# First mixer's values computed ahead of its queries and keys, memory statistics moved forward, and twelve weight chunks in products of 512 columns

## The chip, the cores and the metric

One core of a Trainium2 chip runs the whole program. The metric is device microseconds of one launch: the median of 3 runs was 429.3 us before the change (428.47 to 429.76).

## What is computed

One decoder layer on x, 256 tokens by 1024 channels, all in float32, with a memory of 256 tokens:

```
h = rms_norm(x, g_mix);  proj = h @ w_in                  # qa ka va qb kb vb, 512 columns each
oa = rms_norm(moba_attention(qa, ka, va))                 # 8 heads of 64, causal, T5 bias
ob = rms_norm(softmax(q1 k1) - lam * softmax(q2 k2)) @ v  # 4 differential heads
x += concat(oa, ob) @ w_out
m = rms_norm(mem, g_mem)
x += cross_attention(rms_norm(x), m; w_cq, w_ck, w_cv) @ w_co     # 4 heads of 256
x += (silu(rms_norm(x) @ w_gate) * (rms_norm(x) @ w_up)) @ w_down # inner width 2816
out = rms_norm(x, g_final)
```

## The kernel before

**Split products.** Every large product works on float32 data that is split into two parts of the type fp32r: a high part and the rest. A weight chunk is 1 MB. SP loads it into `wr`; ScalarE (ACT) copies it to `wh`, the high part (L124); VectorE (DVE) subtracts to get `wl`, the rest (L109). That is done in four parts of 512 columns per chunk, called parts below, by `wpart` and `wflush`. Three buffers of each kind exist. The activations have a high and a low tile in the same way. TensorE (PE) then forms high by high, high by low and low by high.

**Two shapes of product.** `ws` (L312) keeps a weight block stationary and streams 256 tokens: six products of 256 columns per k-step, eight k-steps per chunk. `ws2` (L321) has the high and low activations side by side and streams both in one product of 512 columns, and the low weight in one of 256: four products per k-step, the sum of the two halves being taken at evacuation. `as_` (L333) keeps activations stationary and streams 512 weight columns; it makes the values (token-major).

**Stages.** In order: start (load x, transpose it, first chunk); the rest of w_in, as qa ka qa ka, values, qb kb qb kb, values; memory keys (w_ck) and half its values; w_out; w_cq; the other memory values; w_co; gate and up (22 chunks); down (11 chunks). The attention of the first two mixers is spread through the w_in chunks.

**The order of work.** The program is one instruction list per engine, executed in that order. `run` emits the k-steps of a chunk; after each step `tick` advances a counter, the slot, emits the work that the table (`at`, `later`) holds for that slot, and by a credit some parts of later weight chunks. So slot 31 is a place in the lists of all engines, and an instruction that waits holds up whatever stands behind it on its engine. One k-step is one slot. Slot 9 comes after the first step of the second chunk. The GpSimd engine (POOL) builds the bias strip with 32 copies (L234), stores it in DRAM, and issues the transfers of the bias (L256), the gains `gvB`, the lambda vectors `lp`, and the memory (L596); these small steps are also in the table.

**Memory.** `mem_load` fetches it on POOL's queue, `mem_stats` (ACT) squares and sums, `mem_scale` (DVE) multiplies in place, `mem_t` (PE) transposes and splits. They stand in slots 32, 52 to 54, 58 to 59 and 61 to 70.

**Start.** The first chunk (qa) is multiplied unsplit in float32 (`wf`, L377) as its pieces arrive, from `hF`, the gained and transposed x; the split tiles `hH`, `hL` are made from `hF` beside it. Before that six products on a zero tile run (`NWARM`, L197).

The slot mechanism in the code:

```
def tick():
    state["slot"] += 1
    for fn, args in todo.pop(state["slot"], ()):
        fn(*args)
...
at(32, mem_load)
...
for t in range(2):
    at(52 + 2 * t, mem_stats, t)
...
at((61, 64, 67, 70)[j], mem_t, j)
```

Of the kernel before, what the change touches and what calls it, by code (L numbers as in the profile page):

```python
# [24 lines left out]
NWARM = 6  # L25
# [12 lines left out]
def layer(ctx: ExitStack, tc: tile.TileContext, x, mem, mix_norm_g, w_in, moba_out_g, diff_lambda,  # L38
# [14 lines left out]

    def acc(name="acc"):
        return ps.tile([P, 2, 256], FT, name=name, tag="acc", bufs=3)
# [17 lines left out]
    for base in (0, 6):  # L73
        qk = [cols(w_in, base + i) for i in range(4)]
        chunks += [qk[0], qk[2], qk[1], qk[3]]
        v0 = 2 if base == 0 else 5
        chunks += [rows(w_in, 0, v0, 4, 512), rows(w_in, 4, v0, 4, 512)]
# [100 lines left out]
    src, (wa_, wb_) = chunks[0]  # L178
    w0 = wpool.tile([P, wa_, wb_], FT, name="wr", tag="wr")
    for xlo, xn_, k, nk in ((0, 256, 0, 2), (256, 256, 2, 2), (512, 512, 4, 2), (0, 0, 6, 2)):  # L180
        if xn_:
            nc.sync.dma_start(xv[:, :, xlo:xlo + xn_], xsrc[:, :, xlo:xlo + xn_])
        nc.sync.dma_start(w0[:, k:k + nk], src[:, k:k + nk])
    raws[0] = w0
    state["dma"] = 1
    wdma(2)
# [145 lines left out]

    def as_(o, a, ka, ts, w, kw, cs, start, stop):  # L333
# [11 lines left out]
    hH, hL = slot(1), slot(2)  # L345
    h = (hH, hL)
    hF = slot(4, FT)
# [10 lines left out]
    def x_gain(k):  # L358

        b = xb[k // 4 * 2 + k % 2][:, k % 4 // 2, :]  # L360
        if k % 2:
            nc.vector.tensor_scalar(hF[:, k, :], b, g(G_MIX + k), None, op0=OP.mult)
        else:
            nc.scalar.activation(hF[:, k, :], b, AF.Copy, scale=g(G_MIX + k))

    def x_split(j):
        ks = slice(2 * j, 2 * j + 2)
        split(hH[:, ks, :], hL[:, ks, :], hF[:, ks, :])
# [5 lines left out]
    def wf(o, w, k):  # L374

        for c in range(2):
            nc.tensor.matmul(o[:, c, :], w[:, k, c * P:(c + 1) * P], hF[:, k, :], start=k == 0 and c == 0,  # L377
                             stop=k == KT - 1, skip_group_check=True)

    RX = {}  # L380

    def x_stats():
        ss = const.tile([P, 2], FT, name="ssx")
        for t in range(2):
            nc.scalar.activation(sq, xv[:, t, :], AF.Square, accum_out=ss[:, t:t + 1])
        RX[1] = rstd(ss, 2, D, "rx")
# [72 lines left out]
    def v_chunk(m):  # L459
        os_ = as_chunks(h)  # L460
# [110 lines left out]
    def mix_t(e2):  # L571

        if "mix" not in M:
            M["mix"] = (slot(1), slot(2))
        mixH, mixL = M["mix"]
# [53 lines left out]
    for t in range(2):  # L629
        at(52 + 2 * t, mem_stats, t)  # L630
    at(56, mem_rstd)
    for t in range(2):
        at(58 + t, mem_scale, t)
# [4 lines left out]
    at(50, heads, "a")  # L638
# [4 lines left out]
    for j in range(4):  # L643
        at((61, 64, 67, 70)[j], mem_t, j)
# [16 lines left out]
    load_g(gvA, 0, 8)  # L661
    o = acc()
    w0 = raws[0]
    state["part"], state["use"], state["done"], state["slot"] = NP, 1, 1, 8

# [3 lines left out]


    busy(1)
    for k in (0, 1):
        x_t(k)
        x_gain(k)
    busy(1)
    wf(o, w0, 0)
    strips()
    x_split(0)
    for k in (2, 3):
        x_t(k)  # L680
        x_gain(k)
    wf(o, w0, 1)
    x_split(1)
    for k in (4, 5):
        x_t(k)
        x_gain(k)
    for k in (2, 3):
        wf(o, w0, k)
    for k in (6, 7):
        x_t(k)  # L690
        x_gain(k)
    x_split(2)
    x_split(3)
    for k in range(4, KT):
        wf(o, w0, k)
    raws.pop(0)
    wdma()
    wpart()
    wflush()
    x_stats()  # L700
    for q in range(NP - 1):
        wpart()
        wflush()
    state["credit"] = -1.0
    for j in range(4):
        at(9 + j, x_keep, j)
    later(6, qk_evac, o, "qa0", True)
# [3 lines left out]
    v_chunk(0)  # L711
# [4 lines left out]
    v_chunk(1)  # L716
# [13 lines left out]
    def cross_ops():  # L730
        return tuple(cx.tile([P, KT, S], FR, name="c" + n, tag="c" + n) for n in "HL")
# [15 lines left out]
    def pair(a, evac, by_k=False, late_kts=(6, 7)):  # L747

        w0, w1 = wuse(), wuse()
        o = [acc(), acc()]  # L750
        early = [k for k in range(KT) if k not in late_kts]
        if by_k:
            run([st for k in early for i, w in enumerate((w0, w1)) for st in ws_steps(o[i], w, a, [k])],
                done=False)
        else:
            for i, w in enumerate((w0, w1)):
                run(ws_steps(o[i], w, a, early), done=False)
        for i, w in enumerate((w0, w1)):
            run(ws_steps(o[i], w, a, late_kts))
            evac(i, o[i])  # L760

    def single(a, evac, i):
        w = wuse()
        o = acc()
        run(ws_steps(o, w, a))
# [26 lines left out]
    h2 = cross_ops()  # L792
# [248 lines left out]
```

## Time and profile before

| what | value |
|---|---|
| median of 3 runs | 429.3 us |
| the profiled execution, its own time | 429.33 us |
| span of its instructions | 427.6 us |
| PE busy | 416.8 us, 97% |
| PE weight loads busy | 382.8 us, 90% |
| DVE busy | 286.4 us, 67% |
| ACT busy | 251.9 us, 59% |
| POOL busy | 27.8 us, 7% |
| mean granted TensorE clock | 0.999 |

The profiled execution took 1.7 us more than its span, and is as good as equal to the median. Busy time counts each instruction from its start to its end; PE's products overlap, so the distance from one start to the next tells more of their rate than their length. Rows name the line, the engine, the operation, the tile written and the tiles read, then shapes and a count; `b` is any of the large activation buffers, the memory's among them.

### The profile page before, as it was taken

The numbers are of one execution on the slowest core, as the hardware profiler recorded it, in microseconds if no ns is written. First come the engines' busy times: TensorE is split into PE (matmuls) and PEld (weight loads), VectorE is DVE, ScalarE is ACT, GpSimd is POOL, SyncE is SP. The second block draws the span as 40 slices with busy tenths as digits, with TensorE's granted clock in tenths as the row PEclk, the third lists the DMA queues.
The fourth block names the chain that finished last, engine by engine and source line by source line (L and its number), as shares of the span: only waits on it lengthen the run. The fifth ranks groups of instructions, "written<-read, shape, count | busy, mean of one in ns | idle before, by whom it ended". The sixth has DMA issues, their size and how long they took to land.

```text
span 427.6 us, 7261 instructions
## 1 busy us (share of the span) xinstructions
PE 416.8 (97%) x2827; PEld 382.8 (90%) x2827; DVE 286.4 (67%) x575; ACT 251.9 (59%) x542; POOL 27.8 (7%) x75
## 2 busy tenths in 40 slices
PE   7989999999999999999999999999999999999994
PEld 4888899989998999998999999999888888888883
DVE  2687848899487667486649678888776766544423
ACT  3677888789565654465546465555656665433312
POOL 4750200000010000000000100000000000000001
PEclk9999999999999999999999999999999999999999
DMA  7987682335538525334633745546863675555002
GB/s 240 325 248 246 176 247 80 135 110 193 192 102 296 193 100 185 112 109 161 193 131 104 254 153 186 187 154 213 279 196 109 193 290 198 198 196 189 9 0 98
DMA packets 58258, 74.61 MB, mean 174 GB/s; under 512 B 1708, under 2 KB 50128, under 8 KB 58224
## 3 DMA queue, kind: packets, MB, share of 16 engines
q1 hardware_dynamic: 56528, 69.87, 50.0%
q0 software_dynamic: 1344, 3.88, 3.1%
q8 instruction: 22, 0.36, 0.3%
q10 hardware_dynamic: 352, 0.40, 0.3%
q14 instruction: 12, 0.10, 0.1%
HBM read 72.50 MB, written 1.64 MB: 173 GB/s over the span
## 4 chain that ended last, share of the span: by engine, by line
PE 81%; DVE 8%; ACT 5%; issue 3%; DMA 2%; POOL 1%; SPq 0%; POOLq 0%; DVEq 0%; ACTq 0%
PE acc L318 30%; PE y L337 13%; PE acc L337 9%; PE att L318 5%; PE acc L326 5%; PE att L326 5%; PE att L327 3%; PE acc L327 3%; DVE wl L109 2%; DMA b<-in_x_dram 2%; PE oc L863 1%; PE att L819 1%; ACT qs L422 1%; PE att L497 1%; DVE b L439 1%
## 5 line engine op out<-in xcount | busy, mean ns | idle before, releaser
L109 DVE TENSOR_TENSOR wl<-wr,wh 128x512 fp32r<-128x512 f32 x256 | 163.5, 685 | 34.6 <-ACT wh L124 34.2
L124 ACT ACTIVATE wh<-wr 128x512 fp32r<-128x512 f32 x256 | 144.9, 621 | 55.1 <-issue 23.8
L318 PE MATMUL acc<-b,wh 128*128 128x256 f32 x672 | 125.0, 286 | 0.0
L318 PEld LDWEIGHTS acc<-b,wh 128*128 128x128 f32 x672 | 104.5, 191 | 0.3
L318 PE MATMUL acc<-b,wl 128*128 128x256 f32 x336 | 95.3, 284 | 1.3 <-DVE wl L109 1.3
L318 PEld LDWEIGHTS acc<-b,wl 128*128 128x128 f32 x336 | 64.2, 191 | 1.9 <-DVE wl L109 1.9
L337 PE MATMUL y<-wh,b 128*128 128x512 f32 x152 | 49.0, 391 | 0.0
L337 PE MATMUL acc<-wh,b 128*128 128x512 f32 x128 | 40.6, 398 | 0.3 <-ACT wh L124 0.3
L326 PE MATMUL acc<-hs,wh 128*128 128x512 f32 x96 | 37.8, 393 | 0.0
L326 PE MATMUL att<-hs,wh 128*128 128x512 f32 x96 | 37.8, 393 | 0.0
L318 PE MATMUL acc<-cH,wh 128*128 128x256 f32 x128 | 36.4, 284 | 0.0
L318 PE MATMUL acc<-cH,wl 128*128 128x256 f32 x128 | 36.2, 283 | 0.0
L318 PE MATMUL acc<-cL,wh 128*128 128x256 f32 x128 | 36.2, 283 | 0.0
L337 PE MATMUL y<-wl,b 128*128 128x512 f32 x88 | 34.2, 389 | 0.0
L337 PEld LDWEIGHTS y<-wh,b 128*128 128x128 f32 x152 | 28.5, 188 | 5.9
L327 PE MATMUL att<-hs,wl 128*128 128x256 f32 x96 | 27.1, 283 | 0.0
L327 PE MATMUL acc<-hs,wl 128*128 128x256 f32 x96 | 27.1, 283 | 0.0
L337 PEld LDWEIGHTS acc<-wh,b 128*128 128x128 f32 x128 | 22.5, 189 | 4.0 <-ACT wh L124 0.5
L337 PE MATMUL acc<-wl,b 128*128 128x512 f32 x64 | 25.2, 394 | 0.0
L318 PEld LDWEIGHTS acc<-cH,wh 128*128 128x128 f32 x128 | 24.2, 189 | 0.3 <-DVE b L310 0.2
L318 PEld LDWEIGHTS acc<-cL,wh 128*128 128x128 f32 x128 | 24.1, 188 | 0.0
L318 PEld LDWEIGHTS acc<-cH,wl 128*128 128x128 f32 x128 | 24.1, 189 | 0.0
(210 smaller groups left out, 626.0 us busy)
## 6 DMA issues: line engine op xcount, KB each, us to landing
wr<-in_w_gate_dram SPq DMA_DIRECT2D x11, 1024.0 KB, 5.1
wr<-in_w_up_dram SPq DMA_DIRECT2D x11, 1024.0 KB, 5.1
wr<-in_w_down_dram SPq DMA_DIRECT2D x11, 1024.0 KB, 4.9
wr<-in_w_in_dram SPq DMA_DIRECT2D x9, 1024.0 KB, 6.4
wr<-in_w_ck_dram SPq DMA_DIRECT2D x4, 1024.0 KB, 4.7
wr<-in_w_cv_dram SPq DMA_DIRECT2D x4, 1024.0 KB, 5.0
wr<-in_w_out_dram SPq DMA_DIRECT2D x4, 1024.0 KB, 4.9
wr<-in_w_cq_dram SPq DMA_DIRECT2D x4, 1024.0 KB, 4.7
```

What stands on the lines that cost most here:

```text
L109: eng.tensor_tensor(l, t, h, op=OP.subtract)
L124: nc.scalar.activation(h, t, AF.Copy)
L318: nc.tensor.matmul(o[:, c, :], m[:, k, cs], b[:, k, :], start=first and c == 0 and q == 0, stop=last and q == 2, skip_group_check=True)
L326: nc.tensor.matmul(o[c], h[:, k, cs], flat(a[:, k]), start=first, stop=last, skip_group_check=True)
L327: nc.tensor.matmul(o[c][:, 0:256], l[:, k, cs], a[:, k, 0, :], start=False, stop=last, skip_group_check=True)
L337: nc.tensor.matmul(o, m[:, ka, ts], b[:, kw, cs], start=start and q == 0, stop=stop and q == 2, skip_group_check=True)
L422: nc.scalar.activation(qs[to, :, r, :], d[half(r)], AF.Copy)
L439: nc.vector.tensor_tensor(ks[half(1 - r), :, r, :], d[half(r)], ks[half(r), :, r, :], op=OP.subtract)
L497: nc.tensor.transpose(b[:, q * P:(q + 1) * P], e[:, q * P:(q + 1) * P], ident)
L819: nc.tensor.matmul(b[:, t, :], a[:, kt, t * P:(t + 1) * P], k[:, kt, :], start=n == 0, stop=n == 5)
L863: nc.tensor.matmul(o[:, dv, :], v[:, mt, cs], p_[:, mt, :], start=n == 0, stop=n == 5)
```

## The change

Five things change together.

1. The order of the w_in chunks becomes values of the first mixer (two chunks), qa ka qa ka, qb kb qb kb, values of the second mixer. The first chunk is now split like the others, part by part between the pieces of x; there is no unsplit product any more. The order of the loads follows: x's second half now comes behind the whole first chunk.
2. `hH`, `hL` and the other activation pairs that `ws2` reads lie side by side in one tile (`both`).
3. The table: the statistics of x at slots 10 and 11, the gains and lambda ahead of the bias loads on POOL, all eight first bias loads by slot 14, the memory load at slot 16, its statistics at 24 to 26, scaling at 29 and 30, transposes at 31 to 36; the first mixer's logits from slot 37, each head's product with the values nine slots later.
4. w_out and w_co (four chunks each) use `ws2`; the residual is added in four DVE operations of 256 columns instead of one of 512.
5. Gate and up chunks use `ws2` from j = 3 on instead of j = 5 (four chunks more), with the scaled activations `scale_h` prepared sooner.

```
-NWARM = 6
+NWARM = 7
...
+    def both(i, dt=FR):
+        return slots.tile([P, KT, 2, S], dt, name=f"b{i}", tag=f"b{i}")
...
+    chunks += v_rows(2) + qk(0) + qk(6) + v_rows(5)
...
+    xdma(0, 256)
+    wkdma(0, 0)
+    xdma(256, 256)
+    for k in range(1, 4):
+        wkdma(0, k)
+    xdma(512, 512)
+    wkdma(1, 0, 2)
+    wkdma(1, 2, 2)
+    state["dma"] = 2
...
+    def x_split(k):
...
+        nc.scalar.activation(hH[:, k, :], b, AF.Copy, scale=g(G_MIX + k))
+        nc.vector.scalar_tensor_tensor(hL[:, k, :], b, g(G_MIX + k), hH[:, k, :], op0=OP.mult, op1=OP.subtract)
...
-    at(13, x_row)
-    at(24, load_g_rest)
-    at(25, load_lambda)
-    at(9, bias_load, 0, 4)
-    at(10, small_loads)
-    at(20, bias_load, 4, 4)
-    at(32, mem_load)
+    for t in range(2):
+        at(10 + t, x_stats, t)
+    at(18, x_row)
+    at(9, small_loads)
+    at(15, load_g_rest)
+    at(20, load_lambda)
+    at(12, bias_load, 0, 4)
+    at(14, bias_load, 4, 4)
+    at(16, mem_load)
     at(45, bias_load, 8, 4)
+    for t in range(2):
+        at(24 + t, mem_stats, t)
+    at(26, mem_rstd)
+    for t in range(2):
+        at(29 + t, mem_scale, t)
+    for j in range(4):
+        at((31, 33, 35, 36)[j], mem_t, j)
     for i in range(8):
-        at(28 + 4 * i, logits, i, i, f"qa{i // 4}", f"ka{i // 4}", i // 2 % 2, i % 2)
-        at(34 + 4 * i, p_t, i)
-        at((51, 52, 53, 54, 56, 59, 63, 67)[i], pv, i, 0, "a", 64)
...
+        n = 4 * i + (37 if i < 4 else 38)
+        at(n, logits, i, i, f"qa{i // 4}", f"ka{i // 4}", i // 2 % 2, i % 2)
+        at(n + 6, p_t, i)
+        at(n + 9, pv, i, 0, "a", 64)
...
     for k in (0, 1):
         x_t(k)
...
     x_split(0)
+    w_split()
+    x_split(1)
+    busy(2)
+    v_now(0)
     for k in (2, 3):
         x_t(k)
...
+    strips()
+    w_split()
+    v_now(1)
+    w_split()
     x_split(2)
     x_split(3)
+    v_now(2)
     for k in range(4, KT):
...
+        x_t(k)
+    w_split()
+    v_now(3)
+    for k in range(4, KT):
+        x_split(k)
...
+    run(v_steps(wuse(), 1, range(4)))
+    later(1, v_evac, 0, os_)
+    qk_chunk("qa0", True)
...
-            nc.vector.tensor_tensor(xs, o, xs, op=OP.add)
+            for c in range(2):
+                for cs in (slice(0, 256), slice(256, 512)):
+                    nc.vector.tensor_tensor(xs[:, c, :], o[c][:, cs], xs[:, c, :], op=OP.add)
...
-        single(M["mix"], ev, i)
...
+        single(M["mix"], ev, i, ws2_steps, two)
...
-    for j in range(5, NFF // 2):
+    for j in range(3, NFF // 2):
```

`v_now(k)` emits the six products of the values with the k-th piece of the first chunk, `w_split` one part of a weight split, `two` one bank of each of the two accumulator groups.

Three places in the instruction lists are spoken of below. The first is POOL's list from the zero fill of the low-query tile (`b_123`, now `b_124`) to the memory load (`b_93`); first the kernel before:

```order
L239 MEMSET b_123 64x2x256 x4
L281 TENSOR_TENSOR rx<-rxv,mhalf 128x2
L256 DMA bias<-strip_d 32x4x256 x4
L245 DMA gvB<-in_cross_norm_g_dram 8x128
L245 DMA gvB<-in_mem_norm_g_dram 8x128
L245 DMA gvB<-in_ffn_norm_g_dram 8x128
L245 DMA gvB<-in_moba_out_g_dram 4x128
L245 DMA gvB<-in_diff_subln_g_dram 1x16x8
L247 DMA lp<-in_diff_lambda_dram 128x256
L256 DMA bias<-strip_d 32x4x256 x4
L596 DMA b_93<-in_mem_dram 128x2x1024
```

The same stretch of POOL's list with the change:

```order
L259 MEMSET b_124 64x2x256 x4
L265 DMA gvB<-in_cross_norm_g_dram 8x128
L265 DMA gvB<-in_mem_norm_g_dram 8x128
L265 DMA gvB<-in_ffn_norm_g_dram 8x128
L265 DMA gvB<-in_moba_out_g_dram 4x128
L265 DMA gvB<-in_diff_subln_g_dram 1x16x8
L267 DMA lp<-in_diff_lambda_dram 128x256
L301 TENSOR_TENSOR rx<-rxv,mhalf 128x2
L276 DMA bias<-strip_d 32x4x256 x8
L605 DMA b_93<-in_mem_dram 128x2x1024
```

The gains and lambda went ahead of the bias loads; the number of steps ahead of the memory load is the same.

The second is ACT's list of the change around the memory statistics (`ssm` is their sum, `qs` the high part of the first queries, `att` here the transposed memory), with what each waits for:

```order
L409 ACTIVATE ls<-ls 128x2 [waits DVE_49]
L134 ACTIVATE wh<-wr 128x512 x2
L610 ACTIVATE sq,ssm<-b_93 128x1024 [waits DMASW7_49,Activation_49]
L610 ACTIVATE sq,ssm<-b_93 128x1024 [waits Activation_49]
L134 ACTIVATE wh<-wr 128x512 [waits DMAHW6_49]
L432 ACTIVATE qs<-qa_426 64x2x256 [waits DVE_49]
L432 ACTIVATE qs<-qa_426 64x2x256 x3
L134 ACTIVATE wh<-wr 128x512 x2
L323 ACTIVATE b_141<-att,gT 128x256 [waits PE_49]
```

The statistics, which wait for the memory's transfer (DMASW7), moved from behind the first six heads' softmax to a place ahead of the first queries' split and of the fifth chunk's parts.

The third is DVE's and PE's list of the change from the first queries' evacuation (`qa_426`) to the first transposes of the memory, again with the waits; DVE first:

```order
L421 SCALAR_TENSOR_TENSOR qa_426<-acc,RX 128x512 [waits PE_49]
L299 TENSOR_SCALAR rmv<-ssm 128x2 [waits Activation_49]
L438 TENSOR_TENSOR b_124<-qa_426,qs 64x2x256 [waits Activation_49] x2
L119 TENSOR_TENSOR wl<-wr,wh 128x512 [waits DMAHW6_49]
L616 TENSOR_SCALAR b_93<-b_93,rm 128x1024 [waits DMASW7_49,Pool_49]
L119 TENSOR_TENSOR wl<-wr,wh 128x512 [waits Activation_49]
L616 TENSOR_SCALAR b_93<-b_93,rm 128x1024
L325 SCALAR_TENSOR_TENSOR b_142<-att,gT,b_141 128x256 [waits PE_49,Activation_49]
```

and PE, in the last two steps of the first key chunk (slots 31 and 32):

```order
L338 MATMUL acc<-b_129,wh 128x256 x2
L338 MATMUL acc<-b_129,wl 128x256
L317 MATMUL att<-ident,b_93 128x128 [waits DMASW7_49,DVE_49,PE_49]
L317 MATMUL att<-ident,b_93 128x128 [waits DVE_49]
L317 MATMUL att<-ident,b_93 128x128 x2
L338 MATMUL acc<-b_129,wh 128x256 x2
```

The memory's scaling now stands behind the low part of the first queries and one weight part on DVE, and its first transposes on PE before the last step of the first key chunk; before the change they stood some thirty slots later, behind eight heads' logits.

## Rows read from the trace of the kernel before

**Rows 1.** The page, busy time of each engine.

```profile
PE 416.8 (97%) x2827; PEld 382.8 (90%) x2827; DVE 286.4 (67%) x575; ACT 251.9 (59%) x542; POOL 27.8 (7%) x75
```

**Rows 2.** Stretches from the second chunk on: length, then each engine's busy us, clock, DMA.

```profile
16.15:36.07 19.92, 18.59 (x147) 17.78 (x146) 15.62 (x32) 12.93 (x24) 9.01 (x16) 1.00 0.89 272
36.07:52.33 16.26, 15.98 (x88) 13.15 (x87) 12.55 (x35) 14.62 (x41) 2.19 (x4) 1.00 0.58 171
```

**Rows 3.** PE in order of time: start, length; second chunk, first logits, slot 31.

```profile
16.17 0.59 PE L318 MATMUL acc<-b,wh 128*128 128x256 f32 x2
...
33.45 0.22 PE L474 MATMUL att<-b,qs 128*128 128x128 f32 x1
...
33.91 0.40 PE L318 MATMUL acc<-b,wh 128*128 128x256 f32 x2
...
36.07 0.40 PE L318 MATMUL acc<-b,wh 128*128 128x256 f32 x2
```

**Rows 4.** Chain of waits: start, length; value step, four transposes, whole `ws` chunk.

```profile
39.95 1.39 PE acc L337 x6
...
67.66 0.44 PE att L297 x4
...
251.66 5.76 PE att L318 x48
```

**Rows 5.** PE in order of time: first `ws2` product, first instruction after the twelfth chunk.

```profile
291.82 0.39 PE L326 MATMUL acc<-hs,wh 128*128 128x512 f32 x1
...
359.22 0.60 PE L969 MATMUL y<-ident,xT 128*128 128x128 f32 x4
```

**Rows 6.** Groups by line and shape: busy us, mean ns, idle before; adding 512, adding 256.

```profile
L771 DVE TENSOR_TENSOR xT<-acc,xT 128x512 f32<-128x512 f32 x8 | 5.5, 688 | 7.1 <-PE acc L318 7.1
...
L921 DVE TENSOR_TENSOR ag<-acc,ag 128x256 f32<-128x256 f32 x6 | 2.5, 424 | 9.4 <-ACT ag L919 9.4
```

**Rows 7.** ACT and POOL in order of time: first copy, bias strip, POOL's queue.

```profile
5.16 0.47 ACT L364 ACTIVATE b<-xb,gT 128x256 f32<-128x256 f32 x1 [1.92 <-PE xb L355]
...
7.78 4.96 POOL L234 COPY strip<-tT 96x1 f32<-96x1 f32 x32 [3.16 <-DVE tT L228]
13.05 0.85 POOL L235 DMA_DIRECT2D strip_d<-strip  x1 [0.31 <-POOL strip L234]
13.94 2.20 POOL L239 MEMSET b<- 64x512 f32 x4
17.50 0.73 POOL L281 TENSOR_TENSOR rx<-rxv,mhalf 128x2 f32<-128x2 f32 x1 [1.35 <-DVE rxv L279]
...
27.91 1.64 POOL L256 DMA_DIRECT2D bias<-strip_d  x3 [0.26 <-DMA bias<-strip_d]
29.55 0.73 POOL L596 DMA_DIRECT2D b<-in_mem_dram  x1
```

**Rows 8.** DMA issues: count, KB each, median us from issue to landing.

```profile
bias<-strip_d POOLq DMA_DIRECT2D x12, 128.0 KB, 5.8
b<-in_mem_dram POOLq DMA_DIRECT2D x1, 1024.0 KB, 7.6
strip_d<-strip POOLq DMA_DIRECT2D x1, 576.0 KB, 5.4
...
lp<-in_diff_lambda_dram POOLq DMA_DIRECT2D x1, 128.0 KB, 4.3
```

**Rows 9.** ACT and DVE in order of time: statistics of x, splits, scaling of the memory.

```profile
14.82 1.04 ACT L385 ACTIVATE sq<-b 128x1024 f32<-128x1024 f32 x1
...
17.04 2.18 ACT L124 ACTIVATE wh<-wr 128x512 fp32r<-128x512 f32 x4
...
22.61 2.58 ACT L422 ACTIVATE qs<-qa 64x512 fp32r<-64x512 f32 x4 [0.83 <-DVE qa L411]
...
29.97 1.29 DVE L109 TENSOR_TENSOR wl<-wr,wh 128x512 fp32r<-128x512 f32 x2
...
66.33 0.75 DVE L607 TENSOR_SCALAR b<-b,rm 128x1024 f32<-128x1024 f32 x1
```

**Rows 10.** PE's first products in order of time; the last stretch, columns as rows 2.

```profile
1.22 2.74 PE L197 MATMUL clock<-still 128*128 128x512 bf16 x6 [1.22 <-DVE still L194]
...
426.00:427.50 1.50, 0.00 (x0) 0.00 (x0) 0.00 (x0) 0.00 (x0) 0.00 (x0) 0.65 0.00 0
```

More of the change, by code (lines that the diff above doesn't have):

```diff
@@ L71, in rows, with qk, v_rows @@
                 (nk, nc_))
[L73 to L77, printed above, removed]
+    def qk(base):
+        c = [cols(w_in, base + i) for i in range(4)]
+        return [c[0], c[2], c[1], c[3]]
+    def v_rows(v0):
+        return [rows(w_in, 0, v0, 4, 512), rows(w_in, 4, v0, 4, 512)]
+    chunks += v_rows(2) + qk(0) + qk(6) + v_rows(5)
     chunks += [cols(w_ck, i) for i in range(4)]
@@ L331, in ws_steps, with ws2_steps @@
         return [(ws, (o, w, a, k, k == 0, k == KT - 1)) for k in kts]
+    def ws2_steps(o, w, a, kts=range(KT)):
+        return [(ws2, (o, w, a, k, k == 0, k == KT - 1)) for k in kts]
     def as_(o, a, ka, ts, w, kw, cs, start, stop):
@@ L344, in layer @@
     xT = const.tile([P, KT, S], FT, name="xT")
-    hH, hL = slot(1), slot(2)
-    h = (hH, hL)
-    hF = slot(4, FT)
+    h = hH, hL = hl(both(12))
     xb = []
@@ L372, in x_keep, with x_stats @@
         nc.vector.tensor_copy(xT[:, k:k + 3:2, :], xb[j])
[L374 to L378, printed above, removed]
     RX = {}
[L382 to L386, printed above, removed]
+    ssx = const.tile([P, 2], FT, name="ssx")
+    def x_stats(t):
+        nc.scalar.activation(sq, xv[:, t, :], AF.Square, accum_out=ssx[:, t:t + 1])
+        if t:
+            RX[1] = rstd(ssx, 2, D, "rx")
     def x_row():
@@ L573, in mix_t @@
         if "mix" not in M:
-            M["mix"] = (slot(1), slot(2))
-        mixH, mixL = M["mix"]
+            M["mix"] = both(12)
+        mixH, mixL = hl(M["mix"])
         bank = att()
@@ L658, in layer @@
         at((108, 112, 124, 127)[j], mix_t, j)
[L661 to L664, printed above, removed]
     def busy(n):
@@ L744, in layer, with two, pair @@
     mem_v(0)
-    def pair(a, evac, by_k=False, late_kts=(6, 7)):
+    def two():
+        return [flat(acc()), flat(att())]
+    def pair(a, evac, steps, banks, by_k=False, late_kts=(6, 7)):
         w0, w1 = wuse(), wuse()
-        o = [acc(), acc()]
+        o = [banks(), banks()]
         early = [k for k in range(KT) if k not in late_kts]
         if by_k:
-            run([st for k in early for i, w in enumerate((w0, w1)) for st in ws_steps(o[i], w, a, [k])],
+            run([st for k in early for i, w in enumerate((w0, w1)) for st in steps(o[i], w, a, [k])],
                 done=False)
@@ L795, in layer @@
     for i in range(4):
-        single(M["mix"], ev, i)
-    q2 = (slot(1), slot(2))
+        single(M["mix"], ev, i, ws2_steps, two)
+    q2 = hl(both(12))
     def q_evac(i, o):
@@ L943, in layer @@
     box = []
-    pair(h3, lambda i, o: box.append(o))
+    pair(h3, lambda i, o: box.append(o), ws_steps, acc)
+    for i in range(4):
+        later(3 + 10 * i, scale_h, i)
     glu(0, *box)
-    for i in range(4):
-        later(8 + 14 * i, scale_h, i)
-    for j in range(1, 5):
+    for j in (1, 2):
         og, ou = acc(), att()
@@ L953, in layer @@
         glu(j, og, ou)
-    for j in range(5, NFF // 2):
+    for j in range(3, NFF // 2):
         for side in range(2):
             w = wuse()
-            o = [flat(acc()), flat(att())]
-            run([(ws2, (o, w, hs, k, k == 0, k == KT - 1)) for k in range(KT)])
+            o = two()
+            run(ws2_steps(o, w, hs))
             if side == 0:
```

114 lines of the change are left out of this document (42 added, 72 removed).

## The prediction

> **What bounds the kernel now.** I began with the busy times: PE is busy for 416.8 of 427.6 us [rows 1], so the kernel is as long as PE's list plus PE's waits. Then I looked for the waits. From the second chunk on, the first 19.92 us hold 18.59 of PE work and the next 16.26 hold 15.98 [rows 2]: 1.3 + 0.3 = 1.6 us of waits, in the stretch where the split parts are not yet far ahead of PE. A change can therefore gain in three places: the 16.17 us before PE's second chunk [rows 3], those waits, and the number and shape of PE's products. It can lose wherever PE's list meets something that is late. So I read last what the moved steps wait for: POOL's queue and its transfers [rows 7, 8].
>
> The sum below is made on the span (427.6 us); 1.7 us lie around it, and the execution (429.33) stands on the median (429.3). Slots are the table's slots; a k-step of `ws` takes 5.76 / 8 = 0.72 us, one of `as_` 1.39 / 2 = 0.70 [rows 4].
>
> **Products of 512 columns.** Twelve chunks that already go through `ws2` run from 291.82 to 359.22 [rows 5], 5.617 us each; a `ws` chunk takes 5.76 [rows 4]. Twelve more chunks save 12 x 0.143 = 1.7 us. The four adds of the residual cost 4 x 0.42 = 1.7 us of DVE instead of 0.69 [rows 6]; eight chunks make 8 us, which lie beside PE work as long as a chunk (5.6 us) covers its split (4 x 0.65 = 2.6, rows 9), the adds and the gains' products. I cost them at nothing; without that cover it would be 1 us for each of the eight. The earlier `scale_h` and the side-by-side tiles also go at nothing.
>
> **The start.** The unsplit chunk goes; the value chunks come first. PE's warm-up has one product more ahead of the transposes and one less behind the gain's, which cancels. Working down the lists: the high part of k = 0 ends on ACT at 5.63 [rows 7], the first weight part's high copy needs 0.6 more (2.18 / 4 behind others, rows 9), its rest 0.65 on DVE, then four products of 0.23, four transposes (0.44, rows 4) and the strip's transpose: the first strip copy on POOL starts at about 8.9 instead of 7.78 [rows 7]. Carried on in the same way (x's gains and the eight parts of two chunks on ACT), the second value chunk starts at about 15.1, against 16.17 for the second chunk now. Gain 1.1, less about 0.7 for its first low part. From there to slot 49 PE has 8 `ws` steps in place of 8 `as_` steps, +0.2.
>
> **The memory's steps.** This is where I expect the loss. On POOL the steps ahead of the memory load are the same as before; only their waits can shrink. From the first strip copy: 5.27 us to the store of the strip and 3.1 to the end of the zero fills [rows 7], so 8.9 becomes 17.3; six small loads at 0.55 (1.64 / 3) make 20.6; `rx` 0.73, 21.3; eight bias loads at 0.55, 25.7. POOL waits for an older transfer before some issues (the bracket of the row at 27.91), and the first bias load, issued at 21.3, cannot have landed before 25.6 if it takes the 4.3 us of the quickest row of its size (`lp`), or 27.1 at the median of 5.8 [rows 8]. I put the memory's issue at 26.0, 3.5 us sooner than now. Its transfer took 7.6 us [rows 8]; the smaller strip store, 576 KB, took 5.4, which is a lower bound. It lands at 33.6, between 31.4 and 34.9. I take 7.6 because it is the same transfer, behind the same loads.
> The Trainium skill, page "DMA: Bandwidth & Descriptors", section on the anatomy of a GpSimd DMA, fits such a transfer as 2.0 us plus bytes at 436 GB/s: an estimate of 4.4 us here and 2.3 for the 128 KB of `lp`. The trace does not agree (7.6 and 4.3). By the Trainium skill's formula the memory would land at 30.4 and the sum below would be 3.2 us smaller.
>
> ACT reaches the statistics at about 29 and stands there. What is behind them in its list, and in DVE's, then runs one after the other: both statistics 2.22 (14.82 to 17.04), one part's copy 0.55, the first queries' split 2.58 [rows 9]; on DVE the second half of its rest 0.65, a part 0.65, scaling 0.75, a part 0.65, scaling 0.75 [rows 9]. That is 8.8 us: the memory is scaled at 42.4, and PE's list has its transposes at slot 31. PE would be there at about 33 if nothing else held it. It is held once before: at slot 15 it transposes the gains, whose last load is issued near 19.5 and lands near 23.8 at 4.3 us, 3.5 us after PE gets there. That costs nothing as long as PE waits at slot 31 anyway, and up to 3.5 us if it does not.
>
> Now PE passes slot 31 at 36.07 [rows 3], with 427.6 - 36.07 = 391.5 us to go. The changed kernel at that place has done 8 steps of 0.70 and 15 of 0.72, 16.4 us, instead of 23 of 0.72 and one head's logits (0.46, rows 3), 17.0: 0.6 more is left. Left in all: 391.5 + 0.6 + 0.2 - 1.7 = 390.6, less 0.3 of waits after this place that need not come back [rows 2]: 390.3.
>
> **What is late next.** After 42.4 ACT and DVE must clear the transposed memory, two parts, the keys' evacuation, and the keys' split, before the first logits at slot 37. DVE: two pieces of the memory and two parts, two more pieces, the keys (0.65), 4.4 us; ACT: half of what the queries' split takes (1.3), a part, two more pieces (0.47 each, rows 7), 2.8; DVE again: a piece and two rests, 1.8. Some 9.0 us. PE meanwhile has six steps and four sets of transposes: 6 x 0.72 + 4 x 0.44 = 6.1. Wait: 2.9. The first head's product with its values, nine slots later, stands behind the next queries' split on ACT: 0.7 more, an estimate from the same rows.
>
> **Sum.** 42.4 + 390.3 + 2.9 + 0.7 = 436.3 of span, 438.0 us: 2% slower. By the bounds of the landing (31.4 to 34.9) 435.8 to 439.3.
>
> **Rivals.**
> - *The waits behind the memory are hidden.* ACT and DVE catch up while PE does its six steps, or the statistics run faster than I lined them up: 42.4 + 390.3 + 1.7 = 434.4; with the early landing 432.2. For it: DVE is idle for a fifth and ACT for a third of the first of the two stretches now [rows 2]. Against: both lists are in order, and 9.0 stands against 6.1. I give 434.
> - *PE's clock falls in the long wait.* The first six products of the launch took 2.74 us, 0.43 from start to start at 512 columns [rows 10], twice the 0.23 of later ones [rows 4]: the lower of the two levels, 1.2 GHz, until PE had worked for some microseconds; and in the last 1.5 us, after PE has long stopped, the granted clock reads 0.65 [rows 10]. A wait of six or more microseconds at slot 31 may do the same. Then the six steps and the transposes take 12.2 us instead of 6.1; 2.9 of that fall into the next wait, and some of the rest is won back: about 2.5 us more, 440.5. Against: no idle time of that length lies inside the trace. The Trainium skill, page "TensorE: Matmul & The Clock Gate", section on HAM oscillation, has the clock fall to half in idle gaps between bursts of products; the first and the last stretch agree, and no row between shows it.
> - *Nothing waits: faster.* If the memory's issue and transfer are done before ACT is there, the start's gain and the waits' go through: 15.1 + 0.7 + (427.6 - 16.17) + 0.2 - 1.7 - 1.6 = 424.1, or 425.8 us. It decides at the landing: with 8.8 + 390.3 behind it and nothing more, the time of now is met by a landing at 28.5. For it: PE's list is otherwise shorter and the values' order frees DVE early. Against: 28.5 is 2.5 us after the issue, and the quickest row takes 4.3 for an eighth of the bytes. A share goes to my start being wrong.
> - *The wider products save nothing* because their evacuation holds PE or the rate is that of the old shape: 1.7 more than the sum, 439.7. For it only the four adds; against it twelve chunks in the trace that do it.
>
> **How the numbers follow.** Forecast 0.40 (438.0), clock 0.18 (440.5), hidden waits 0.16 (434), wide products idle 0.04 (439.7): slower 0.78. Faster 0.16 (425.8). Between them, a partial hit of both within 0.3% of 429.3 (about what a measurement of this kernel can tell from no change): 0.06. The range must hold 0.8: it takes in the slower cases but for their upper end, and the same case, 429.0 to 441.5. Without the last it would be 431.5 to 441.5, the forecast's own bounds being 435.8 to 439.3.
>
> **What would show it.** In the changed profile: the memory's transfer landing between 31 and 35; ACT idle before its first square of the memory, put down to that transfer; PE idle before the memory's first transposes, 5 to 7 us, until 41 to 44; a second wait of some 3 us before the first logits; a first one at the gains' transpose of up to 3.5. Gate and up from j = 3 at 5.62 us per chunk. The forecast is wrong if PE passes the memory's transposes before 37, if ACT finds the memory landed, or if a chunk of w_out or w_co takes 5.76 or more.

## The result and the profile after

The changed kernel takes 447.67 us (median of 4 runs, 446.01 to 448.94) where the kernel before, run beside it on the same chip, takes 428.88: 1.0436 times as long, interval 1.04 to 1.0473. The forecast was 438.0 with a range of 429.0 to 441.5. The direction was right; the loss of 18.8 us is more than twice the 8.7 forecast, and the time lies outside the range.

The profiled execution took 448.78 us, its span 446.7. On the page, busy time first and then the granted clock in 40 slices:

```profile
span 446.7 us, 6949 instructions
...
PE 422.1 (94%) x2652; PEld 379.7 (85%) x2652; DVE 296.2 (66%) x607; ACT 257.9 (58%) x554; POOL 27.9 (6%) x75
...
PEclk9989889999999999999999999979999999999999
```

Against [rows 1] PE has 175 instructions fewer and yet more busy time, and is no longer busy for nearly the whole span: 24.6 us are not covered, 10.8 before. The clock, at full level in both stretches of [rows 2], falls in the first quarter and once more at slice 27. PE's waits, the largest first:

```profile
PE acc L346 <- DVE hs L325: 4.4, 1, 4.4
PE att L317 <- issue: 3.7, 1, 3.7
PE gp L289 <- DMA gvB<-in_diff_subln_g_dram: 3.5, 1, 3.5
PE att L483 <- DVE b L449: 3.1, 1, 3.1
...
PE att L317 <- DVE b L616: 0.9, 1, 0.9
```

Line 317 is the memory's transposes (3.7 + 0.9), 289 the gains' transpose, 483 the first logits. `issue` means that the profile names no releaser; DVE's first scaling of the memory ends at 41.4, 0.1 before these transposes start. These three were forecast. The first row was not: it is the wide gate product, waiting for the last quarter of its scaled operand `hs`. In the chain that ended last (start, length, what) the first 43 us read as forecast:

```profile
9.16 5.45 POOL strip L254 x32
14.92 0.85 POOL strip_d L255
...
21.10 0.77 POOL rx L301
...
26.62 7.94 DMA b<-in_mem_dram
34.65 1.16 ACT sq L610 x2
...
42.02 0.68 DVE b L616
42.74 0.90 PE att L317 x3
```

The forecast had the strip's first copy at 8.9, `rx` at 20.6, the memory's issue at 26.0, its landing at 33.6 and its last scaling done at 42.4; they came at 9.2, 21.1, 26.6, 34.6 and 42.7. ACT stood for the landing, as forecast:

```profile
34.65 1.06 ACT L610 ACTIVATE sq<-b 128x1024 f32<-128x1024 f32 x1 [4.68 <-DMA b<-in_mem_dram]
```

The four stretches in which the granted clock was 0.50, that is 1.2 GHz (columns as in rows 2):

```profile
25.65:29.07 3.42, 3.42 (x19) 3.42 (x18) 2.68 (x9) 2.04 (x6) 1.70 (x3) 0.50 0.81 226
42.72:46.13 3.41, 3.39 (x16) 3.40 (x17) 1.58 (x4) 1.88 (x4) 0.00 (x0) 0.50 0.01 2
52.96:59.79 6.83, 6.25 (x30) 6.28 (x30) 4.45 (x11) 2.60 (x8) 0.00 (x0) 0.50 0.08 13
288.48:295.31 6.83, 5.07 (x15) 4.31 (x16) 5.80 (x12) 5.19 (x11) 0.00 (x0) 0.50 0.33 97
```

Each belongs to one of the four waits. The first begins 1.4 us after PE is back at work (24.2), the second as it comes back (42.7); the third and the fourth begin 0.6 and 1.8 us before the wait ends (53.5 and 290.2). What a stretch costs is half of PE's work in it, for instance of 5.07 us in the fourth. Last, PE's first product of w_out and its first of w_cq, which come four wide chunks apart:

```profile
153.51 0.39 PE L346 MATMUL acc<-b,wh 128*128 128x512 f32 x1
...
176.12 0.40 PE L338 MATMUL acc<-cHL,wh 128*128 128x256 f32 x2
```

22.61 / 4 = 5.65 us a chunk, against 5.76 with 256 columns [rows 4]: the wide products do what they were forecast to do.

### The profile page after: what moved, and what is told of

The parts are those of the page before. It is cut to its first block, busy times and chain, and to the rows that moved or that the text cites. A ratio compares the mean times of both kernels' runs of the same rounds, so it can differ in the third digit from the quotient of the medians.

```text
span 446.7 us, 6949 instructions
## 1 busy us (share of the span) xinstructions
PE 422.1 (94%) x2652; PEld 379.7 (85%) x2652; DVE 296.2 (66%) x607; ACT 257.9 (58%) x554; POOL 27.9 (6%) x75
## 4 chain that ended last, share of the span: by engine, by line
PE 80%; DVE 6%; ACT 4%; POOL 4%; issue 2%; DMA 2%; POOLq 0%; DVEq 0%; ACTq 0%
PE acc L338 21%; PE y L360 12%; PE acc L346 10%; PE att L346 10%; PE acc L360 8%; PE acc L347 5%; PE att L347 5%; DVE wl L119 2%; DMA b<-in_mem_dram 2%; PE att L837 1%; PE oc L881 1%; POOL strip L254 1%; PE att L483 1%; POOL bias L276 1%; PE att L506 1%
## 5 line engine op out<-in xcount | busy, mean ns | idle before, releaser
L338 PE MATMUL acc<-b,wh 128*128 128x256 f32 x512 | 100.7, 296 | 0.0
L338 PEld LDWEIGHTS acc<-b,wh 128*128 128x128 f32 x512 | 83.4, 200 | 0.2
L338 PE MATMUL acc<-b,wl 128*128 128x256 f32 x256 | 74.6, 291 | 0.0
L346 PE MATMUL acc<-hs,wh 128*128 128x512 f32 x128 | 51.5, 402 | 4.4 <-DVE hs L325 4.4
L347 PE MATMUL acc<-hs,wl 128*128 128x256 f32 x128 | 36.7, 287 | 0.0
L347 PE MATMUL att<-hs,wl 128*128 128x256 f32 x128 | 36.6, 286 | 0.0
L346 PEld LDWEIGHTS acc<-hs,wh 128*128 128x128 f32 x128 | 24.6, 192 | 10.3 <-DVE hs L325 4.7
L346 PEld LDWEIGHTS att<-hs,wh 128*128 128x128 f32 x128 | 24.6, 192 | 5.8
L347 PEld LDWEIGHTS acc<-hs,wl 128*128 128x128 f32 x128 | 24.6, 193 | 0.0
L347 PEld LDWEIGHTS att<-hs,wl 128*128 128x128 f32 x128 | 24.6, 192 | 0.0
L338 PE MATMUL acc<-cHL,wh 128*128 128x256 f32 x128 | 23.4, 283 | 0.0
L338 PEld LDWEIGHTS acc<-cHL,wh 128*128 128x128 f32 x128 | 19.6, 189 | 0.0
```

The lines of the kernel that those rows point to most:

```text
L338: nc.tensor.matmul(o[:, c, :], m[:, k, cs], b[:, k, :], start=first and c == 0 and q == 0, stop=last and q == 2, skip_group_check=True)
L346: nc.tensor.matmul(o[c], h[:, k, cs], flat(a[:, k]), start=first, stop=last, skip_group_check=True)
L347: nc.tensor.matmul(o[c][:, 0:256], l[:, k, cs], a[:, k, 0, :], start=False, stop=last, skip_group_check=True)
```

## The experiments

| run | edit, to the changed kernel if not said | us | ratio to before, interval |
|---|---|---|---|
| changed kernel | | 447.67 | 1.0436 [1.04, 1.0473] |
| 1 | memory's steps at the slots of before | 435.54 | 1.0166 [1.0149, 1.0183] |
| 2 | wide gate and up from j = 5, `scale_h` as before | 441.94 | 1.0313 [1.0295, 1.0331] |
| 3 | 1 and 2 | 429.42 | 1.0010 [0.9984, 1.0035] |
| 4 | waits filled with products | 443.99 | 1.0359 [1.0337, 1.038] |
| 5 | 3, gains at 24 | 425.76 | 0.9939 [0.9927, 0.9951] |
| 6 | `scale_h` at 3 + 9 i | 442.05 | 1.0323 [1.0304, 1.0341] |
| 7 | before, attention outputs wide | 427.14 | 0.9975 [0.995, 1.0] |
| 8 | 1, 6, gains at 24 | 426.52 | 0.9955 [0.9943, 0.9967] |
| 9 | 2, gains at 24 | 443.86 | 1.0349 [1.0316, 1.0382] |
| 10 | 9, memory loaded at slot 9 by ACT's queue | 434.44 | 1.0125 [1.0094, 1.0156] |
| 11 | 5, memory's statistics and scaling early | 436.27 | 1.0170 [1.0143, 1.0197] |
| 12 | 5, all first logits at 38 + 4 i | 424.31 | 0.9893 [0.9872, 0.9915] |

**1 to 3: which part of the change loses what.** The theory: every loss is a wait that the change made, with the half clock that follows it. Its rival: the waits alone.

```diff
-        at(24 + t, mem_stats, t)
+        at(52 + 2 * t, mem_stats, t)
-    at(26, mem_rstd)
+    at(56, mem_rstd)
-        at(29 + t, mem_scale, t)
+        at(58 + t, mem_scale, t)
-        at((31, 33, 35, 36)[j], mem_t, j)
+        at((61, 64, 67, 70)[j], mem_t, j)
```

> The changed kernel (447.7 us) with the memory's statistics, scaling and transposes back at the slots of before (52/54, 56, 58/59, 61 to 70); its load stays early. Theory A, waits and the clock that falls after each of them: goes are the 5.0 us before the memory's first transposes, the 3.2 us before the first logits, and half of the two stretches at half clock behind these (3.4 and 6.8 us, 1.7 and 3.1 us of work). 447.7 - 5.0 - 3.2 - 1.7 - 3.1 = 434.7 us, 433.5 to 436.5; the clock is at half only behind the gains' wait and at 288 us. Theory B, the waits alone count: 447.7 - 8.2 = 439.5 us. Theory C, the transposes only change place and meet other waits at slots 61 to 70: 444 us or more.

```diff
-    for i in range(4):
-        later(3 + 10 * i, scale_h, i)
     glu(0, *box)
-    for j in (1, 2):
+    for i in range(4):
+        later(8 + 14 * i, scale_h, i)
+    for j in range(1, 5):
-    for j in range(3, NFF // 2):
+    for j in range(5, NFF // 2):
```

> The changed kernel (447.7 us) with four gate and up chunks (j = 3 and 4) back in products of 256 columns, and the scaling of the operand back at slots 8 + 14 i after the first gate. Four chunks lose 0.143 us each, +0.6. Theory A: the 4.5 us wait inside the first wide gate chunk at 285.6 us goes, and with it the half clock of 288.5 to 295.3 us (3.4 us of work): 447.7 - 4.5 - 3.4 + 0.6 = 440.4 us, 439.5 to 441.5. Theory B, the wait alone: 443.8 us. Theory C, that wait is taken back later by weights or by the scalar engine, nothing gained: 447.5 to 448.5 us.

> Both edits together: memory back at the slots of before, and wide gate and up products from j = 5. What is left of the change is the value chunk ahead of queries and keys, the gains' transpose at slot 15, the earlier loads, and wide products for the attention outputs. Theory A: 447.7 - 13.0 - 7.3 = 427.4 us, 426 to 429; half clock only behind the gains' wait at about 25 us. Theory B (waits alone): 447.7 - 8.2 - 3.9 = 435.6 us.

Measured: 12.1 us less, 5.7 less, and both together 18.3 less, so the parts add up and the result equals the kernel before. The first lies in the range of waits with clock (434.7 expected, 439.5 for waits alone). The second is only just nearer to it (440.4 against 443.8) and outside its range, and the third stands 2 us above its number (427.4), also outside, but 6 below waits alone. One reason is on record: the second expectation took 3.4 us for the clock behind the `hs` wait, and the stretch holds only 5.07 us of work, so 2.5. The largest of PE's waits in the third is now the gains; the others take 1.3 us or less:

```profile
PE gp L289 <- DMA gvB<-in_diff_subln_g_dram: 3.3, 1, 3.3
```

**4: the clock by itself.** The waits stay, but PE works in them.

```diff
+    def fill(n):
+        b = obank("fill")
+        for _ in range(n):
+            nc.tensor.matmul(b, still[:, 0:P], still, start=True, stop=True)
+    at(15, fill, 14)
+    at(31, fill, 22)
+    at(37, fill, 13)
...
+            if (j, side) == (3, 0):
+                later(6, fill, 19)
             run(ws2_steps(o, w, hs))
```

> The changed kernel (447.7 us) with products of 512 columns on zeros that nobody reads, put on the tensor engine in each of the four waits: 14 ahead of the gains' transpose, 22 ahead of the memory's first transposes, 13 ahead of the first logits, 19 ahead of the k = 6 step of the first wide gate chunk. Each run of them is about as long as the wait there, so the waits stay and the engine is busy in them. Theory A, the clock falls because the engine stood: no stretch at half clock, and the work lost in three of the four comes back (1.7 + 3.1 + 3.4 us; that behind the gains' wait lies before the memory's wait, whose end is set elsewhere): 447.7 - 8.2 = 439.5 us, 438.5 to 441.5. Theory B, the half clock costs nothing beside the waits: 447.5 to 449.5 us, as the products are added work. Theory C, the clock falls from something else than standing: the stretches at half remain, 447 to 450 us.

The half clock is gone; the same four stretches in this kernel:

```profile
25.65:29.07 3.42, 3.42 (x31) 3.42 (x30) 3.08 (x11) 2.60 (x6) 1.66 (x3) 1.00 0.71 188
42.72:46.13 3.41, 2.64 (x23) 2.64 (x24) 1.90 (x5) 2.06 (x5) 0.00 (x0) 1.00 0.02 7
52.96:59.79 6.83, 6.83 (x58) 6.83 (x59) 6.06 (x17) 4.57 (x13) 0.00 (x0) 1.00 0.16 40
288.48:295.31 6.83, 6.83 (x41) 5.96 (x40) 5.97 (x12) 5.16 (x12) 0.00 (x0) 1.00 0.76 236
```

So it was PE's standing that brought it, and theories B and C fall. But 443.99 is 3.7 us less and not the 8.2 expected, and it lies outside the range given. The two profiled spans (446.7 and 441.3) are 5.4 apart and show where the expectation was too high. The first logits come at 52.88 in place of 53.54, 0.7 sooner where 1.7 was expected. Here the memory's transfer took 8.7 us against 7.9, and the second group of its transposes starts 0.75 us later (43.49 against 42.74). From there to the first logits it is 9.4 us in place of 10.8, so full clock was worth 1.4 and the later landing took half of it back. From the logits to the first w_out product it is 97.6 in place of 100.0, with 3.1 expected, and from that product to the first of the down projection, in the last row below, 224.1 in place of 226.5, with 3.4 expected: the fourth stretch had begun inside the wait. 0.7 + 2.4 + 2.4 is the 5.4 between the spans, with rounding. Between the medians it is 3.7; the changed kernel's traced execution (448.78) is one of its two longer ones.

```profile
43.49 0.55 PE L317 MATMUL att<-ident,b 128*128 128x128 f32 x3 [0.94 <-DVE b L616]
...
52.88 0.30 PE L483 MATMUL att<-b,qs 128*128 128x128 f32 x1 [0.41 <-DVE b L449]
...
150.46 0.39 PE L346 MATMUL acc<-b,wh 128*128 128x512 f32 x1
...
L360 PE MATMUL y<-wh,b x152: 389/389/477, 374.6 to 434.2; 128*128 128x512 f32 x152
```

The changed kernel's rows for the logits and the down projection (the last: median ns, first and last start):

```profile
53.54 0.45 PE L483 MATMUL att<-b,qs 128*128 128x128 f32 x1 [3.12 <-DVE b L449]
...
L360 PE MATMUL y<-wh,b x152: 387/389/476, 380.0 to 439.6; 128*128 128x512 f32 x152
```

**5: the gains' transpose.**

```diff
-    at(15, load_g_rest)
-    at(20, load_lambda)
+    at(24, load_g_rest)
+    at(25, load_lambda)
```

> The third experiment (memory and wide gate and up products back, 429.4 us) with the gains' transpose and the lambda back from slots 15 and 20 to 24 and 25. Theory A: the 3.3 us wait for the gains and the half of the 3.4 us at half clock behind it go: 429.4 - 3.3 - 1.7 = 424.4 us, 423.5 to 425.5, with no stretch at half clock before the end. This is then what the values ahead of queries and keys and the wide attention outputs bring. Theory B, the later transpose waits elsewhere, for its bank or its copy: 427.5 to 429.5 us.

3.7 us less than the third run, 3.0 by the ratios to the kernel before; 5.0 was expected, and 425.76 lies just outside theory A's range. The 3.3 us and the half clock are gone; a new wait of 0.8 us stands at the first logits, which PE now reaches earlier. This kernel beats the kernel before by 2.5 us. If the wide outputs give 1.1 of them, as in run 7, some 1.4 are left for all that this kernel otherwise keeps of the change, the values' order first; no run has that order alone.

**6: why `hs` was late.** In the changed kernel DVE, in order of time around PE's wait (285.6 to 290.2):

```profile
280.45 0.89 DVE L325 SCALAR_TENSOR_TENSOR hs<-z,gT,hs 128x256 fp32r<-128x256 f32 x2 [0.58 <-ACT hs L323]
281.25 3.09 DVE L119 TENSOR_TENSOR wl<-wr,wh 128x512 fp32r<-128x512 f32 x5
284.25 0.69 DVE L920 TENSOR_TENSOR t<-acc,R 128x512 f32<-128x512 f32 x1
...
287.83 0.69 DVE L330 TENSOR_TENSOR b<-ag,b 128x512 fp32r<-128x512 f32 x1 [0.69 <-ACT b L329]
288.44 0.68 DVE L932 TENSOR_TENSOR z<-xT,R 128x512 f32<-128x512 f32 x1
289.70 0.88 DVE L325 SCALAR_TENSOR_TENSOR hs<-z,gT,hs 128x256 fp32r<-128x256 f32 x2 [0.58 <-ACT hs L323]
```

`scale_h(2)` is done at 281.3. The fourth starts at 288.4: between them stand five weight parts and the whole `glu(2)`, which goes to and fro between DVE and ACT and leaves both idle in turn. The table put `scale_h(3)` at slot 33 after the pair, one tick behind `glu(2)` at 32 and five ahead of the step that reads it. One number moves it ahead:

```diff
-        later(3 + 10 * i, scale_h, i)
+        later(3 + 9 * i, scale_h, i)
```

> The changed kernel (447.7 us), wide gate and up products from j = 3 kept, the operand's scaling at slots 3 + 9 i in place of 3 + 10 i: the fourth stands at slot 30, ahead of the third gate and up evacuation at 32, in place of behind it. Theory A, the wait came from that place in the vector engine's order: the 4.5 us wait and its clock go as in the second experiment, and the four wide chunks stay: 441.9 - 0.6 = 441.3 us, 440.5 to 442.3. Theory B, the vector engine has too much to do by then in any order, and the wait moves to the next evacuation: 443.5 to 446 us. Theory C, no change: 447 to 448.5 us.

442.05: the order was the cause. In this kernel the fourth scaling stands ahead of `glu(2)`'s line 920, and PE waits only 0.9 us later on, for a weight part that now stands behind `glu(2)`:

```profile
284.09 0.68 DVE L932 TENSOR_TENSOR z<-xT,R 128x512 f32<-128x512 f32 x1
285.35 0.89 DVE L325 SCALAR_TENSOR_TENSOR hs<-z,gT,hs 128x256 fp32r<-128x256 f32 x2 [0.58 <-ACT hs L323]
...
286.75 0.68 DVE L920 TENSOR_TENSOR t<-acc,R 128x512 f32<-128x512 f32 x1
```

This trace shows two things more. PE's wait at the gains is 3.0 us here, and the granted clock stays at 1.00 behind it, from 24 to 36 us. PE is then at slot 31 sooner and stands there longer, 6.3 + 0.8 us in place of 3.7 + 0.9; the memory landed 0.6 us later here, and the first logits came 0.5 later (54.0). So what the half clock behind the gains cost in the changed kernel lay within the memory's wait.

```profile
PE att L317 <- issue: 6.3, 1, 6.3
...
PE gp L289 <- DMA gvB<-in_diff_subln_g_dram: 3.0, 1, 3.0
```

**7: the wide outputs alone**, on the kernel before, with the same side-by-side tiles and the residual's four adds.

```diff
-        single(M["mix"], ev, i)
+        single(M["mix"], ev, i, ws2_steps, two)
...
-    pair(oT, ev, True)
+    pair(oT[0], ev, ws2_steps, two, True)
...
-        single(oT, ev, i)
+        single(oT[0], ev, i, ws2_steps, two)
```

> The kernel before (428.4 us) with the eight chunks of the two attention outputs alone in products of 512 columns, and the tiles that lie side by side for them. Theory A: 8 x 0.143 = 1.1 us less, 427.3 us, 426.9 to 427.8. Theory B, the residual's four adds per chunk in place of one come late for the next split or hold a bank, and give it back: 428.3 to 429.5 us.

1.1 us less, as expected of eight chunks, so the adds cost nothing that shows; the interval just reaches no change. Two of the twelve executions took 431.4 and 431.75. The latter is the traced one: the last gains load is issued late, behind a bias load, and PE stands at the gains' transpose, at slot 24 as before, with half clock behind it. That wait can thus also come in the order of the kernel before.

```profile
PE gp L275 <- issue: 3.3, 1, 3.3
```

```profile
PEclk9997999999999999999999999999999999999998
```

**8: all three waits mended, everything else kept.** The edits of runs 1, 5 and 6 together.

> The changed kernel with its three waits taken away and all else kept: memory's statistics, scaling and transposes at the slots of before, gains' transpose and lambda at 24 and 25, scaling of the wide operand at 3 + 9 i. Values ahead of queries and keys, wide outputs, wide gate and up from j = 3 stay. Theory A: 424.4 (expected of the kernel with wide products from j = 5) - 4 x 0.143 = 423.8 us, 422.8 to 425.0, under the kernel before by about 1%. Theory B, the wait for the wide operand stays at slots 3 + 9 i: 427 to 431 us.

426.52 misses theory A by 2.7 us and is no better than run 5, which has four chunks fewer in wide products. The wait of 0.9 us for a weight part (below, L347) is still there. From the first w_out product to the down projection it takes 220.7 us and run 5 220.1; four chunks in wide products should have made it 219.5. The sooner scaling costs 1.2 us there, this wait the larger part, and in no run did these four chunks gain anything.

```profile
274.19 0.39 PE L347 MATMUL acc<-hs,wl 128*128 128x256 f32 x1 [0.91 <-DVE wl L119]
```

**9 to 11: what holds the memory.** Run 9 has the gains' edit of run 5 on run 2. Run 10 adds:

```diff
-        nc.gpsimd.dma_start(memv, mem[0].rearrange("(t p) c -> p t c", p=P))
+        nc.scalar.dma_start(memv, mem[0].rearrange("(t p) c -> p t c", p=P))
-    at(16, mem_load)
+    at(9, mem_load)
```

> The second experiment (memory's steps at the changed slots, wide products from j = 5, 441.9 us) with the gains' transpose and the lambda at slots 24 and 25. Theory A, the end of the memory's wait is set by the landing and the chain of vector and scalar work behind it, so what the tensor engine gains ahead of slot 31 it stands longer there: the 3.7 us at the gains go and the wait at slot 31 grows by as much, from 4.7 to about 9 us: 441.9 us, 441 to 443. Theory B, the waits add up: 441.9 - 3.7 = 438.2 us.

> The kernel of the run before this one with the memory's load issued at slot 9 by the scalar engine's queue in place of slot 16 by GpSimd's, so that it is there before the statistics are due. Theory A, the landing is the cause: the chain of 8.8 us then starts when the scalar engine comes to slot 24, at about 27 us, the memory is scaled at about 35.5 in place of 42.5, and the wait at slot 31 (reached at 32.5) is 3 us in place of 9: 441.9 - 7 = 435 us, 433 to 437. Theory B, the engines' chain is the cause whatever the landing: 441 to 443 us. Theory C, one MB more in the first stage takes the weights' place in the transfers: new waits for weights, 438 to 445 us.

Taking the gains' wait away made run 2 1.9 us slower, not 3.7 faster. PE's wait at the memory, 3.8 + 0.9 in run 2, is 11.56 and 0.79 here. The granted clock is at half for 13.65 us; 7.45 of them lie inside the wait and 6.2 behind its end:

```profile
44.33 0.47 PE L317 MATMUL att<-ident,b 128*128 128x128 f32 x1 [11.56 <-DVE b L616]
45.59 0.90 PE L317 MATMUL att<-ident,b 128*128 128x128 f32 x3 [0.79 <-DVE b L616]
```

```profile
36.88:50.53 13.65, 5.41 (x25) 5.12 (x26) 7.61 (x18) 8.92 (x18) 0.72 (x1) 0.51 0.07 26
```

That the wait grows by what PE gains ahead of it was expected. That it grew further was not, and 443.86 is above theory A's range: the transfer took 10.3 us here and 8.1 in run 2. With the memory loaded sooner (run 10; 6.9 us, landed before the statistics are due) 9.4 of the 443.9 us go, and PE waits there 1.98 + 0.93:

```profile
b<-in_mem_dram ACTq DMA_DIRECT2D x1, 1024.0 KB, 6.9
```

```profile
34.76 0.33 PE L317 MATMUL att<-ident,b 128*128 128x128 f32 x1 [1.98 <-DVE b L616]
...
46.84 0.45 PE L483 MATMUL att<-b,qs 128*128 128x128 f32 x1 [3.12 <-DVE b L449]
```

So the landing set the length of that wait. Even so the early steps cost. The same 3.1 us stand at the first logits, and the clock falls behind both places (slices 4 and 5 below), so run 10 is 8.7 us slower than run 5, which differs in the memory's load and steps alone.

```profile
PEclk9998699999999999999999999999999999999999
```

Run 11 keeps run 5's late transposes but takes the early statistics and scaling:

```diff
-        at(52 + 2 * t, mem_stats, t)
+        at(24 + t, mem_stats, t)
-    at(56, mem_rstd)
+    at(26, mem_rstd)
-        at(58 + t, mem_scale, t)
+        at(29 + t, mem_scale, t)
```

> The fourth experiment (425.8 us) with the memory's statistics, rstd and scaling at the changed slots 24 to 30, its transposes at 61 to 70: half of the change to the memory. Theory A, only the transposes' place in the tensor engine's order costs time: 425.5 to 427 us, though the scalar engine stands about 7 us until the memory lands. Theory B, that stand reaches the tensor engine, by the weight parts behind it or by the keys' split ahead of the first logits: a wait of 3 to 6 us near slot 37, 429 to 433 us.

10.5 us slower than run 5, more than theory B gave (429 to 433). ACT stood 10.61 us for the landing, and PE waited for the weight parts behind it:

```profile
36.12 1.06 ACT L610 ACTIVATE sq<-b 128x1024 f32<-128x1024 f32 x1 [10.61 <-DMA b<-in_mem_dram]
```

```profile
39.66 0.79 PE L338 MATMUL acc<-b,wh 128*128 128x256 f32 x2 [6.18 <-ACT wh L134]
42.91 0.58 PE L338 MATMUL acc<-b,wl 128*128 128x256 f32 x1 [2.46 <-DVE wl L119]
```

So the transposes' place in PE's list is not what matters most: the statistics, queued on ACT ahead of weight parts, hold PE by themselves.

**12: one slot at the first logits.**

```diff
-        n = 4 * i + (37 if i < 4 else 38)
+        n = 4 * i + 38
```

(on run 5)

> The fourth experiment (425.8 us) with the first four logits one slot later (38 + 4 i in place of 37 + 4 i), like the other four. Theory A: the 0.9 us wait ahead of the first logits shrinks by one slot of 0.72 us and nothing takes its place: 425.1 us, 424.7 to 425.5. Theory B, the wait was cover for weight parts that are then late: no change, 425.6 to 426.1 us.

424.31, the fastest of all and 1.1% under the kernel before, and better than theory A's range. Its traced execution shows the wait at 0.6 where run 5 has 0.8, so the mechanism explains little of the 1.45 us between the medians; where the rest comes from isn't shown.

## Why the prediction was right in direction and wrong in size

**Right.** POOL's queue, the start (the second value chunk at 15.1 forecast, 15.4 in the trace), the stand of ACT for the landing, up to 3.5 us at the gains (3.5), the two waits of PE that follow from the memory, and the wide chunks. Run 10 shows that the landing was the cause, as argued. The 0.7 us at the first product with the values did not come.

The Trainium skill, page "DMA: Bandwidth & Descriptors", section on the anatomy of a GpSimd DMA, would have had 4.4 us for this transfer, an estimate from its fit. The traces do not agree: they show 7.2 to 10.3 on that queue.

**Right partly by luck.** The memory was scaled at 42.7 where 42.4 was forecast, but it landed 1.0 us later (34.6 against 33.6) and the chain behind it took 8.1 us and not 8.8. PE stood 4.6 us at slot 31, less than the 5 to 7 forecast, for it came there at 37.8, after half clock. The 3.1 us at the first logits against 2.9 are the difference of two sizes that were both too small: 10.8 us for the engines' work against 9.0, and 7.7 for PE's against 6.1, as PE's steps ran in part at half clock. DVE's share of the 9.0, 4.4 us, had no row for the memory's pieces; what it lists takes 3.7 in the trace, and the rest of the time the engines wait for one another. The rival "nothing waits: faster" gave 425.8 for the case without those waits. Run 5, which takes them away, measured 425.76, but with four wide chunks fewer than that case has and a wait of 0.8 us at the first logits that it had not, so the match is no proof of that sum.

**The step that failed** is the sentence "The earlier `scale_h` and the side-by-side tiles also go at nothing", in the part on the products of 512 columns. The tiles cost nothing that shows (run 7). The earlier `scale_h` cost 5.6 us, its half clock included (run 6), for it stood behind `glu(2)` on DVE: PE waited 4.4 us for it. With that mended the time is 442.05, still above the range, and what is left over is the clock's. Before the change `scale_h(3)` was emitted twenty slots ahead of the step that reads it (50 against 70); with the change PE's list asks for it four chunks sooner, and five slots were left (33 against 38). The forecast named no cover for it and looked at no row of DVE's order there, which was to be had before the change ran: slot 33 against slot 32.

**The second miss is the clock.** It was a rival at 0.18, with a place only behind the memory's wait and a price of 2.5 us. It came with each of the four waits, at 3.1 us as at 4.4, and cost 5.4 us between the profiled spans, 6.2 with the later landing taken out, and 3.7 between the medians (run 4). The forecast and this rival were written as alternatives; both happened. Of the two signs that the rival rested on, the first was inferred from the rate of the products alone: in these first microseconds the granted clock of the kernel before reads 1.00.

The Trainium skill, page "TensorE: Matmul & The Clock Gate", section on HAM oscillation, has the clock fall to half in idle gaps between bursts. The four stretches at 0.50 and run 4, where they are gone, agree with it; the gap of 3.0 us in run 6 brought no fall.

**How the 10.4 us between the forecast span (436.3) and the real one (446.7) divide.** The forecast put the first logits at 42.4 + 6.1 + 2.9 = 51.4; they came at 53.5, 2.1 later: 0.3 from the scaling, 1.4 from half clock (run 4), and 0.4 because the engines' work takes 9.4 us even at full clock. From there to w_out 1.3 are lost: 2.4 at half clock, less 1.1 that the forecast had too much, the 0.7 at the values among it. From the first w_out product to the down projection it took 226.5 us. Run 5, with products of 256 columns in four chunks more and no wait there, has 220.1, so 219.5 with the four: 7.0 over, of which run 4 gives 2.4 to the clock and leaves 4.6 to the `hs` wait. In all, the clock took 6.2 and the wait 4.6; what else was missed nearly cancels.

Against the kernel before, going by runs 3 and 5, the loss is 18.3 for the memory's steps and the operand's scaling, 3.7 for the gains, less the 2.5 that run 5 gains: 19.5 of 18.8. Such a chain of runs must close but for the scatter of the kernel before. What need not have come out is that runs 1 and 2 apart (12.1 + 5.7 = 17.8) make nearly the 18.3 of run 3. The 3.7 at the gains are a loss only where the memory's wait is gone; with it in place, taking them away gained nothing (run 9), as the prediction had said.

## What to carry to other kernels

When work is moved earlier, find for each moved step the instruction that stands in front of it on its own engine, and the first one behind it that another engine needs: a step that waits for a transfer holds everything behind it in its queue, and a step put one tick behind a long evacuation is as late as that evacuation. Price an idle stretch of PE with the half clock that may come with it, but by the work that lies in that stretch, and count it as nothing where a later wait with an end of its own covers it. A wait taken away ahead of another that something else ends gains nothing. And count what a moved step costs against what it makes room for: the four more chunks in wide products would save 0.6 us, and even with the scaling in time they did not pay (run 8).

## What the runs showed of the hardware that was not expected

- In the changed kernel waits of 3.1 to 4.6 us each came with 3.4 or 6.8 us at half clock, which began between 1.8 us before the end of the wait and 1.4 after it. In run 6 no fall came with a wait of 3.0 us; in run 10 one came behind two waits of 1.98 and 0.93 us with one product between them. Products that nobody reads, put into the waits, kept the clock at full and were worth 3.7 us of 447.7.
- The same 1 MB load on GpSimd's queue, issued between 26.1 and 27.3 us, took 7.9 to 8.9 us in the six kernels with the gains at slot 15 and 8.9 to 10.3 in the five with them at 24, in one trace each. From 26 to 34.5 us the busy share of the DMA engines was 0.94 in the changed kernel, 0.96 in run 2 and 1.03 in run 9, where PE is not held up ahead, but also 1.04 in run 5, where the load took 8.9 us. That the weights' loads are in the way would fit in part; it was not tried.
